# A fused two-layer matmul with scheduled fast products: nine sum slots in place of eight, 21 y slots in place of 23, new orders, and one block's x sums kept in DRAM for the second pass

## The chip, the cores and the metric

One core of one Trainium2 chip. The metric is the device time of one execution in microseconds (us), the median of the runs shown.

## The reference

```python
batch, m, k, h, n = 16, 512, 768, 3072, 768        # x, w1, b1, w2 in float32
y = np.maximum(np.matmul(x, w1) + b1, 0)
return np.matmul(y, w2).astype(np.float32)
```

With the batch flattened, x is 8192 x 768, w1 is 768 x 3072 and w2 is 3072 x 768.

## The kernel before

**Tiling.** The hidden dimension 3072 is cut into two *chunks* of 1536. Rows of x are cut into eight *blocks* of 1024. One *iteration* handles one block with one chunk: iterations 0 to 7 run chunk one over blocks 0 to 7, iterations 8 to 15 chunk two over blocks 7, 0, 1, ... 6 (`block`). Chunk one writes its part of the output to DRAM; chunk two adds its part there, with stores that accumulate, and only POOL's queue can issue those.

**Fast products.** Both layers use a bilinear scheme with fewer products than a plain split. Each operand is cut into pieces, sums and differences of pieces are formed first, products of these are taken, and the products are combined into the outputs. Stage one (`add_first`, matmuls at L980) multiplies sums of x by sums of w1: 40 products of six matmuls an iteration. The first block alone is done plainly (L890). Stage two (`add_second`, matmuls at L1109) multiplies sums of y by sums of w2: 26 products of six matmuls. The tables `X_SUMS`, `Y_SUMS`, `W1_SUMS` and `W2_SUMS` name each sum (result, two sources, sign), and `X_FUSE` and `Y_FUSE` say which two consecutive sums go as one DVE instruction of double width. `FIRST_ORDER` and `SECOND_ORDER` give the order of the products (`SWITCH_ORDER` for iterations 7 and 8, `LAST_ORDER` for the last one).

**After a product.** A chain of products ends in PSUM. It becomes an output ("out"), a *kept sum* in SBUF ("sum"), or the start of another chain in PSUM ("seed"). Where a chain stands alone, ACT copies it (L1016, L1020, L1120); where a kept sum is added, DVE does it (L1023, L1026, L1031, L1126). Kept sums of both stages, and outputs of stage two on their way to DRAM, share the slots of the tile `s`, `S_SLOTS` = 8 of 3 KB a partition. A slot is free again when the last reader is through, and for an output that is the landing of its store. The tile `y` has `Y_SLOTS` = 23 slots of 1.5 KB: 16 for the pieces of y and seven for sums; a further sum takes the slot of a sum or a piece whose last product is done (`place_between`).

**Split outputs.** An output that is a chain plus a kept sum can be made in two ways. Usually DVE adds the two (L1126) and one store is issued. Where it is *split* (`SPLIT` names output 6 always; `APART` names iterations, here 7 and 8, in which all such outputs are split), the kept sum is stored by itself (L1161), ACT copies the chain, and a second, accumulating store adds it (L1158).

**x.** POOL loads half a block of x with a cast to fp16 (L634, 768 KB), SP transposes it into x slots by DMA (`add_turns`, 8 a block), and DVE forms the x sums (L735). In the iteration in which a block's x is transposed, ACT squares its rows once for a range check (`add_square_x`, L694); similar squares check w1 and w2 (`add_stats`). At the end of the check one matmul counts the values in range (`add_check`), DVE makes a flag (L1281), and all engines read it for a branch behind the fast path.

**Order of the work.** `plan` adds every operation to a `Graph` with its engine, an assumed duration and what it reads and writes. `Graph.run` plays that through with these assumed durations and fixes for each engine the order in which its instructions are emitted; on the chip only data dependences remain. A task marked `idle` (squares) is put where the engine has room before its next urgent task. A store's `lat` is the time that the planner assumes until its slot is free. On each engine, POOL's and SP's DMA queues among them, instructions go strictly in the emitted order.

Of the kernel before, what the change touches and what calls it, by code (L numbers as in the profile page):

```python
# [10 lines left out]
FP16 = mybir.dt.float16  # L11
# [7 lines left out]
P = 128  # L19
# [11 lines left out]

X_SUMS = ((17, 6, 1, -1), (20, 7, 5, -1), (12, 2, 0, -1), (23, 4, 6, -1), (10, 3, 1, -1), (16, 1,
    0, -1), (21, 7, 1, -1), (8, 4, 5, -1), (15, 2, 1, -1), (14, 3, 5, -1), (11, 2, 5, -1), (22, 6,
    7, -1), (19, 4, 2, -1), (9, 6, 5, -1), (13, 0, 6, -1), (18, 3, 2, -1))
FIRST_U = (8, 9, 21, 18, 2, 13, 20, 19, 1, 14, 10, 17, 11, 22, 6, 12, 5, 23, 15, 16)
W1_SUMS = ((6, 2, 5, 1), (15, 3, 5, -1), (7, 0, 1, 1), (13, 7, 2, -1), (8, 6, 4, -1), (9, 6, 3,
    -1), (12, 9, 0, -1), (14, 7, 9, -1), (10, 8, 7, -1), (16, 3, 10, -1), (17, 1, 8, -1), (11, 5,
    4, -1))
FIRST_V = (2, 9, 4, 11, 17, 1, 3, 1, 16, 4, 3, 14, 8, 15, 12, 0, 6, 0, 10, 13)
# [28 lines left out]
FIRST_SEEDS = (16, None, None, 13, 12, 14, None, None, None)  # L68
FIRST_ORDER = (16, 20, 36, 0, 12, 4, 1, 24, 8, 7, 18, 28, 9, 15, 10, 21, 38, 3, 32, 35, 30, 27,
    14, 29, 34, 17, 37, 31, 23, 6, 11, 25, 26, 2, 5, 39, 13, 22, 19, 33)  # L70
SWITCH_ORDER = (36, 16, 20, 12, 4, 8, 9, 0, 7, 18, 28, 24, 15, 10, 21, 38, 3, 32, 35, 30, 27, 1,
    29, 14, 34, 37, 11, 31, 6, 17, 22, 25, 26, 23, 2, 5, 39, 13, 33, 19)

Y_SUMS = ((35, 6, 7, 1), (21, 1, 3, 1), (19, 10, 11, 1), (16, 0, 12, 1), (20, 8, 9, 1), (28, 2,
# [4 lines left out]
SECOND_U = (36, 38, 25, 27, 28, 3, 16, 23, 13, 11, 14, 39, 20, 35, 34, 17, 42, 41, 29, 33, 43, 40,  # L79
    18, 22, 32, 31)  # L80
W2_SUMS = ((18, 5, 1, -1), (9, 5, 7, -1), (10, 4, 5, -1), (12, 2, 0, -1), (23, 12, 9, -1), (11, 3,
    2, -1), (8, 2, 6, -1), (20, 9, 6, -1), (13, 1, 10, 1), (17, 1, 11, 1), (24, 11, 10, -1), (15,
    8, 3, -1), (14, 9, 1, -1), (16, 8, 0, -1), (22, 16, 4, -1), (25, 0, 13, 1), (19, 7, 15, -1),
    (21, 3, 14, -1))
SECOND_V = (8, 10, 13, 14, 16, 21, 22, 23, 1, 19, 6, 25, 4, 12, 3, 20, 11, 0, 15, 9, 4, 18, 17,
    24, 0, 7)
W2_NEG = (1, 6)
SECOND_OPS = {
    0: (1, 1, 9, 1, 'out', 2, None),
    1: (4, 1, 14, 1, 'out', 3, None),  # L90
    2: (0, 1, None, None, 'out', 0, None),
    3: (4, -1, 12, 1, 'out', 1, None),
    4: (2, -1, 11, 1, 'out', 4, None),
    5: (2, 1, 20, 1, 'out', 5, None),
    6: (3, 1, 19, 1, 'out', 6, None),
# [30 lines left out]
LAST_ORDER = (13, 15, 4, 17, 10, 12, 18, 8, 2, 0, 3, 14, 1, 19, 21, 23, 25, 11, 16, 7, 22, 9, 5,  # L126
    6, 24, 20)
# [3 lines left out]

X_FUSE = (0, 2)
Y_FUSE = (7, 9, 13, 18, 26)

S_SLOTS, Y_SLOTS = 8, 23

# [145 lines left out]
class Graph:  # L282
# [5 lines left out]
    ENGINES = ("PE", "DVE", "ACT", "POOL", "SP")  # L288
    HOLD = 2.0
    CROSS = {"PE": 0.15, "DVE": 0.08, "ACT": 0.08, "POOL": 0.1, "SP": 0.1}  # L290

# [87 lines left out]
    def run(self, begin=0.0, lookahead=0.2, ahead=5):  # L379
# [37 lines left out]
        while left:  # L417
            best = None
            for e in self.ENGINES:
                cands = []  # L420
                low = 1e9
                for t in avail[e]:
# [25 lines left out]
                    if t.idle and start < t.due + drift:  # L448
                        d = demand[e]
                        while first[e] < len(d) and d[first[e]].end is not None:  # L450
                            first[e] += 1
                        if first[e] < len(d) and start + t.ns > d[first[e]].late + drift + 0.3:
                            continue
# [60 lines left out]
SPLIT = (6,)  # L514
APART = (7, 8)

STATS = ((1, 2, 3, 4, 5, 6, 7), (2, 3, 4))


class Fast:  # L520
# [43 lines left out]
    def open(self, ctx, tc):  # L564
# [15 lines left out]
        self.w1dram = dram.tile([P, self.NG, 6, 3, 2 * P], FP16, name="w1d")  # L580
        self.w2dram = dram.tile([P, 8, 3, self.NH], FP16, name="w2d")


# [41 lines left out]
    def block(self, it):  # L625

        return it if it < self.NSB else (it - 1) % self.NSB

# [61 lines left out]
    def add_square_x(self, it, s, due=None):  # L690
        i = self.block(it) * 8 + s

        def square():
            self.nc.scalar.activation(out=self.xn[:, s, :], in_=self.xn[:, s, :],  # L694
                                      func=ACTF.Square,
                                      accum_out=self.stat[:, self.stat_at["x"] + i:][:, 0:1])
        self.g.add("ACT", 850, square, writes=[("xn", s), ("stat", "x", i)], due=due, idle=True)

# [76 lines left out]
    def add_stat_w1(self, c, g, i, after=()):  # L775
# [9 lines left out]
        for n in range(2):  # L785
            self.g.add("ACT", 935, lambda n=n: square(n), reads=[] if n else [("w1", g, slot)],
                       writes=["junk"] + ([("stat", "w1", at)] if n else []), idle=True,
                       after=after)

    def add_stat_w2(self, c, i, after=()):  # L790
        slot = self.w2s[c][i]
        for n, (h0, h1) in enumerate(((0, 2), (2, 3))):
            at = self.stat_at["w2"] + c * 16 + 2 * i + n

            def square(h0=h0, h1=h1, at=at):
# [3 lines left out]
                    accum_out=self.stat[:, at:at + 1])  # L799
            self.g.add("ACT", 520 if n else 935, square,  # L800
                       reads=[("w2", slot, h) for h in range(h0, h1)],
# [283 lines left out]
    def add_second(self, it):  # L1085
# [104 lines left out]
        for kind, n in steps:  # L1190
# [21 lines left out]
            if what == "out":  # L1212
# [9 lines left out]
                elif n in apart:  # L1222
                    assert b == 1
                    self.g.add("POOL" if c else "SP", 1375 if c else 100,
                               lambda to=to, u=u: store_sum(to, u), reads=[kept[u]],
                               writes=[("out", self.block(it), to)], lat=9.0 if it == 0 else 6.5)
                    engine = "ACT"
# [68 lines left out]
    def plan(self):  # L1296
# [51 lines left out]
    def iteration_end(self, it):  # L1348
# [4 lines left out]
        self.add_second(it)  # L1353
        if it + 1 < NIT and it + 1 != NSB:
            self.add_turns(it + 1)
            if (it + 1 < NSB) == (self.block(it + 1) > 1):
                for s in range(8):
                    self.add_square_x(it + 1, s)
            to = it + 2 + (it + 2 == NSB)
            if to < NIT:  # L1360
                for half in range(2):
                    self.add_load_x(to, half)
            self.add_x_sums()
        if it == NSB - 1:
            slot = self.w2s[1]
# [74 lines left out]
```

## Time and profile before

| | us |
|---|---|
| Median of 3 runs (lowest, highest) | 875.22 (874.09, 876.23) |
| The profiled execution's own time | 878.86 |
| Its span | 877.3 |
| TensorE (PE) busy | 852.7 |
| VectorE (DVE) busy | 755.1 |
| ScalarE (ACT) busy | 556.5 |
| GpSimd (POOL) busy | 154.5 |
| Stage one's matmuls (L980) busy | 399.7 |
| Stage two's matmuls (L1109) busy | 417.5 |
| DMA moved | 124.99 MB, mean 142 GB/s |

Busy times are unions of instruction times on one engine, in one profiled execution. Matmuls are pipelined, so a busy TensorE need not be at its peak. "Idle before" is an engine's idle time just before an instruction, and the name behind it is what ended it. A DMA's landing is counted from its issue.

### The profile page before, as it was taken

To read this page: it belongs to the slowest core of one execution; us is meant where nothing else is said; L and a number is where in the kernel's file an instruction comes from. 1 tells how busy PE (TensorE), PEld (TensorE's weight loads), DVE (VectorE), ACT (ScalarE), POOL (GpSimd) and SP (SyncE) were. 2 spreads that over 40 slices of the span, in tenths; PEclk is the share of its full clock that TensorE was granted. 3 is DMA by queue.
4 is the path that set the end of the run, shared out by engine and by line. 5 is a ranking of instruction groups with operands and counts; after the bars stand their busy time and mean duration, and the time that the engine had idled before them with its cause. 6 is when DMAs were issued, how large, how long until landed. Compare 5 with 4: busy or idle time off the path is not lost. (4 is left out here: it accounts for less than half of the span.)

```text
span 877.3 us, 16551 instructions
## 1 busy us (share of the span) xinstructions
PE 852.7 (97%) x6381; PEld 624.9 (71%) x6381; DVE 755.1 (86%) x1207; ACT 556.5 (63%) x1066; POOL 154.5 (18%) x168
## 2 busy tenths in 40 slices
PE   8999999999999999999999799999999999999996
PEld 7558778586776868778586575776858677586873
DVE  4899988979889898998989589799798988889896
ACT  5757857678576775847858467675856636355452
POOL 5210020201002010000113502314022140401301
PEclk9999999999999999999999999999999999999998
DMA  9994596875849576592976996989778896873827
GB/s 211 198 187 125 98 228 108 150 180 96 206 74 202 131 107 174 91 268 66 253 135 99 201 142 105 158 119 140 116 117 143 126 145 111 127 124 55 145 74 163
DMA packets 168247, 124.99 MB, mean 142 GB/s; under 512 B 93645, under 2 KB 166629, under 8 KB 168165
## 3 DMA queue, kind: packets, MB, share of 16 engines
q0 software_dynamic: 54928, 66.46, 49.1%
q1 hardware_dynamic: 112768, 56.45, 26.8%
q8 instruction: 50, 0.82, 0.4%
q10 hardware_dynamic: 468, 1.00, 0.3%
q14 instruction: 33, 0.26, 0.1%
HBM read 72.76 MB, written 66.06 MB: 158 GB/s over the span
## 5 line engine op out<-in xcount | busy, mean ns | idle before, releaser
L1109 PE MATMUL ps<-v,y 128*128 128x384 f16 x2496 | 417.5, 326 | 4.8 <-ACT s L1120 4.0
L980 PE MATMUL ps<-x,v 128*128 128x256 f16 x3600 | 399.7, 273 | 9.7 <-DVE ps L1031 5.8
L980 PEld LDWEIGHTS <-v 128*128 128x128 f16 x3600 | 352.3, 98 | 56.3 <-issue 14.1
L1109 PEld LDWEIGHTS <-y 128*128 128x128 f16 x2496 | 243.5, 98 | 174.3 <-issue 16.1
L953 DVE TENSOR_TENSOR y<-y 128x768 f16<-128x768 f16 (+1 forms) x368 | 225.4, 641 | 10.4 <-ACT y L899 0.2
L1023 DVE CUSTOM_DVE_ANT_0 y<-ps,s 128x512 f16<-128x512 f32 x240 | 159.2, 687 | 60.4 <-ACT s L1020 36.2
L1120 ACT ACTIVATE s<-ps 128x768 f32<-128x768 f32 x171 | 138.4, 810 | 93.4 <-PE ps L1109 80.4
L1020 ACT ACTIVATE s<-ps,bt 128x256 f32<-128x256 f32 x180 | 75.3, 472 | 80.7 <-PE ps L980 55.8
L735 DVE TENSOR_TENSOR x<-x 128x768 f16<-128x768 f16 (+1 forms) x196 | 113.4, 607 | 1.3 <-DVE x L735 1.0
L1158 POOL DMA_DIRECT2D out_dram<-s x73 | 88.0, 1412 | 145.8 <-ACT s L1120 90.6
L634 POOL DMA_DIRECT2D xn<-in_x_dram x30 | 23.6, 789 | 426.9 <-ACT xn L694 289.7
L1120 ACT ACTIVATE ps<-ps 128x768 f32<-128x768 f32 x80 | 63.6, 795 | 47.2 <-DVE s L1126 32.7
L1126 DVE TENSOR_TENSOR s<-ps,s 128x768 f32<-128x768 f32 x85 | 80.6, 957 | 5.9 <-PE ps L1109 3.2
L1020 ACT ACTIVATE y<-ps,bt 128x256 f16<-128x256 f32 x180 | 72.0, 474 | 16.3 <-PE ps L980 16.3
L1126 DVE TENSOR_TENSOR s<-s,ps 128x768 f32<-128x768 f32 x59 | 56.2, 952 | 8.5 <-PE ps L1109 8.0
L694 ACT ACTIVATE xn<-xn 128x768 f16<-128x768 f16 x64 | 53.5, 843 | 2.4 <-DMA x<-xn 2.4
L1016 ACT ACTIVATE ps<-ps 128x512 f32<-128x512 f32 x60 | 34.2, 591 | 27.1 <-DVE y L1023 26.9
L1020 ACT ACTIVATE ps<-ps,bt 128x256 f32<-128x256 f32 x60 | 26.7, 448 | 28.1 <-PE ps L980 26.9
L1161 POOL DMA_DIRECT2D out_dram<-s x14 | 17.1, 1300 | 126.4 <-ACT s L1120 126.4
L890 PE MATMUL ps<-x,v 128*128 128x256 f16 (+1 forms) x216 | 32.1, 308 | 1.0 <-DMA v<-in_w_dram 0.6
L1026 DVE SCALAR_TENSOR_TENSOR s<-ps,bt,s 128x256 f32<-128x256 f32 x60 | 26.2, 478 | 5.1 <-PE ps L980 3.0
L890 PEld LDWEIGHTS <-v 128*128 128x128 f16 x216 | 20.9, 98 | 11.4 <-DMA v<-in_w_dram 0.9
(58 smaller groups left out, 300.2 us busy)
## 6 DMA issues: line engine op xcount, KB each, us to landing
out_dram<-s POOLq DMA_DIRECT2D x87, 384.0 KB, 8.4
out_dram<-s SPq DMA_DIRECT2D x68, 384.0 KB, 6.6
xn<-in_x_dram POOLq DMA_DIRECT2D x28, 768.0 KB, 8.0
v<-in_w_dram POOLq DMA_DIRECT2D x6, 384.0 KB, 10.7
v<-in_w_dram POOLq DMA_DIRECT2D x12, 192.0 KB, 9.1
w1d<-in_w_dram POOLq DMA_DIRECT2D x6, 384.0 KB, 18.6
w2d<-in_w_dram POOLq DMA_DIRECT2D x12, 192.0 KB, 14.3
v<-w1d SPq DMA_DIRECT2D x12, 192.0 KB, 4.3
```

The costliest lines, as they stand in the source:

```text
L694: self.nc.scalar.activation(out=self.xn[:, s, :], in_=self.xn[:, s, :], func=ACTF.Square, accum_out=self.stat[:, self.stat_at["x"] + i:][: ...
L735: self.nc.vector.tensor_tensor(out=self.two(x, out), in0=self.two(x, in0), in1=self.two(x, in1), op=ALU.add if sign > 0 else ALU.subtract)
L890: nc.tensor.matmul(self.ps[:, ps.at[0], cols], lhsT=self.v1[:, gi, 2 * h + k2, k, j * P:(j + 1) * P], rhs=rhs, start=(k2 == 0 and k == 0), ...
L953: self.nc.vector.tensor_tensor(out=self.two(self.y, out), in0=self.two(self.y, in0), in1=self.two(self.y, in1), op=ALU.add if sign > 0 els ...
L980: nc.tensor.matmul(self.ps[:, at, j * self.QM:(j + 1) * self.QM], lhsT=self.v1[:, gi, self.w1s[c][gi][FIRST_V[p]], k, j * P:(j + 1) * P], ...
L1016: nc.scalar.activation(out=out, in_=ps, scale=float(a), func=func if kind == "out" else ACTF.Copy)
L1020: nc.scalar.activation(out=out[:, j], in_=ps[:, j], func=func, scale=float(a), bias=beta(j))
L1023: nc.vector._custom_dve(TENSOR_ADD_SAT, out=out, in0=ps, in1=s, s0=F_MAX, s1=0.0)
L1109: nc.tensor.matmul(self.ps[:, bank[ch].at[j], 0:NH], lhsT=self.y[:, ys[SECOND_U[p]], m0:m0 + P], rhs=self.v2[:, slot[SECOND_V[p]], h, :], ...
L1120: nc.scalar.activation(out=out, in_=ps, func=ACTF.Copy, scale=float(a))
L1126: engine.tensor_tensor(out=out, in0=in0, in1=in1, op=ALU.add if a == b else ALU.subtract)
L1158: nc.gpsimd.dma_start(out=rows, in_=out, accum_op=ALU.add)
```

## The change

- `S_SLOTS` 8 becomes 9, `Y_SLOTS` 23 becomes 21; the SBUF space is the same.
- New orders of the products, and of the sums of x, y, w1 and w2; the products and the operations stay the same but for names. `X_FUSE` loses one pair, so that a block's x sums are 15 instructions in place of 14; `Y_FUSE` has five pairs as before.
- `APART` becomes iterations 0 and 7.
- Chunk two runs over the blocks 7, 2, 0, 1, 3, 4, 5, 6. Block 2's x slots, pieces and sums, are stored to DRAM in iteration 1 (`add_keep_x`, 20 DMAs on SP) and loaded in iteration 8 (`add_kept_x`, 20 DMAs on SP), in place of its second load, transposes and sums. The x of iteration 10 is loaded at the end of iteration 6.
- The squares of blocks 0 and 1 fall into iterations 9 and 10 instead of 8 and 9. The checks of the weights in chunk two spread over four iterations instead of three, and the final count and the flag come one iteration later.
- The planner's assumed durations for squares and its assumed `lat` of stores are larger. `NEXT` = 1 looks at one urgent task, as before.

```diff
-X_SUMS = ((17, 6, 1, -1), (20, 7, 5, -1), (12, 2, 0, -1), ...
+X_SUMS = ((15, 2, 1, -1), (21, 7, 1, -1), (16, 1, 0, -1), ...
...
-FIRST_ORDER = (16, 20, 36, 0, 12, 4, 1, 24, 8, 7, 18, 28, ...
+FIRST_ORDER = (16, 0, 12, 36, 20, 8, 4, 7, 9, 1, 18, 24, ...
...
-SECOND_ORDER = (13, 15, 4, 17, 10, 8, 18, 12, 3, 0, 1, 2, 14, 23, 19, 21, 11, 25, 7, 16, 22, 5, 6,
-    9, 24, 20)
+SECOND_ORDER = (13, 15, 4, 17, 10, 8, 18, 12, 3, 0, 1, 14, 2, 19, 23, 21, 11, 16, 25, 7, 9, 22, 6,
+    5, 24, 20)
...
-X_FUSE = (0, 2)
-Y_FUSE = (7, 9, 13, 18, 26)
-S_SLOTS, Y_SLOTS = 8, 23
+X_FUSE = (0,)
+Y_FUSE = (7, 10, 12, 19, 25)
+S_SLOTS, Y_SLOTS = 9, 21
...
-APART = (7, 8)
-STATS = ((1, 2, 3, 4, 5, 6, 7), (2, 3, 4))
+APART = (0, 7)
+KEPT = (2,)
+SECOND_CHUNK = (7, 2, 0, 1, 3, 4, 5, 6)
+STATS = ((1, 2, 3, 4, 5, 6, 7), (2, 3, 4, 5))
...
-        return it if it < self.NSB else (it - 1) % self.NSB
+        return it if it < self.NSB else SECOND_CHUNK[it - self.NSB]
+    def kept(self, it):
+        return self.NSB < it < self.NIT and self.block(it) in KEPT
...
-        self.g.add("ACT", 850, square, ...
+        self.g.add("ACT", 1035, square, ...
+    def add_keep_x(self, it):
+        n = KEPT.index(self.block(it))
+        for a in self.x_slots():
+            self.g.add("SP", 100, lambda a=a: self.nc.sync.dma_start(
+                out=self.xdram[:, n, a], in_=self.x[:, a]), lat=4.0, ...
+    def add_kept_x(self, it):
+        n = KEPT.index(self.block(it))
+        for a in self.x_slots():
+            self.g.add("SP", 600, lambda a=a: self.nc.sync.dma_start(
+                out=self.x[:, a], in_=self.xdram[:, n, a]), lat=4.0, ...
...
-                           lat=9.0 if it == 0 else 3.5 if direct else 6.5)
+                           lat=3.5 if direct else 9.0)
...
-            if it == NSB + 5:
+            if it == NSB + 6:
                 later = self.add_check()
-            elif it == NSB + 6:
+            elif it == NSB + 7:
                 later()
-            elif it == NSB + 7:
                 g.add("SP", 10, self.load_flag, reads=["flag"])
...
-        if it + 1 < NIT and it + 1 != NSB:
+        if self.kept(it + 1):
+            self.add_kept_x(it + 1)
+        elif it + 1 < NIT and it + 1 != NSB:
             self.add_turns(it + 1)
...
-            to = it + 2 + (it + 2 == NSB)
+            to = [n for n in range(it + 2, NIT) if n != NSB and not self.kept(n)]
...
             self.add_x_sums()
+            if it + 1 < NSB and self.block(it + 1) in KEPT:
+                self.add_keep_x(it + 1)
```

More of the change, by code (lines that the diff above doesn't have):

```diff
@@ L451, in run @@
                             first[e] += 1
-                        if first[e] < len(d) and start + t.ns > d[first[e]].late + drift + 0.3:
+                        end, fits = start + t.ns, True
+                        for n in range(first[e], min(first[e] + self.NEXT, len(d))):
+                            if d[n].end is None:
+                                fits &= end <= d[n].late + drift + 0.3
+                                end += d[n].ns
+                        if not fits:
                             continue
@@ L696, in square, with x_slots @@
                                       accum_out=self.stat[:, self.stat_at["x"] + i:][:, 0:1])
-        self.g.add("ACT", 850, square, writes=[("xn", s), ("stat", "x", i)], due=due, idle=True)
+        self.g.add("ACT", 1035, square, writes=[("xn", s), ("stat", "x", i)], due=due, idle=True)
+    def x_slots(self):
+        last = {FIRST_U[p % len(FIRST_U)]: n for n, p in enumerate(FIRST_ORDER)}
+        return [self.xs[v] for v in sorted(last, key=lambda v: last[v])]
+    def add_keep_x(self, it):
+        n = KEPT.index(self.block(it))
+        for a in self.x_slots():
+            self.g.add("SP", 100, lambda a=a: self.nc.sync.dma_start(
+                out=self.xdram[:, n, a], in_=self.x[:, a]), lat=4.0,
+                reads=[("x", a, h) for h in range(2)], writes=[("xd", n, a)])
+    def add_kept_x(self, it):
+        n = KEPT.index(self.block(it))
+        for a in self.x_slots():
+            self.g.add("SP", 600, lambda a=a: self.nc.sync.dma_start(
+                out=self.x[:, a], in_=self.xdram[:, n, a]), lat=4.0, reads=[("xd", n, a)],
+                writes=[("x", a, h) for h in range(2)])
     def sums_of(self, table, slots, fused):
@@ L785, in add_stat_w1 @@
         for n in range(2):
-            self.g.add("ACT", 935, lambda n=n: square(n), reads=[] if n else [("w1", g, slot)],
+            self.g.add("ACT", 1040 if n else 845, lambda n=n: square(n), reads=[] if n else [("w1", g, slot)],
                        writes=["junk"] + ([("stat", "w1", at)] if n else []), idle=True,
@@ L1225, in add_second @@
                                lambda to=to, u=u: store_sum(to, u), reads=[kept[u]],
-                               writes=[("out", self.block(it), to)], lat=9.0 if it == 0 else 6.5)
+                               writes=[("out", self.block(it), to)], lat=9.0)
                     engine = "ACT"
```

58 lines of the change are left out of this document (30 added, 28 removed), and 8 rows, old and new, of the table Y_SUMS.

## The prediction

> **What bounds the kernel now.** I read the page, then TensorE's timeline over the span, the waits, ACT's and POOL's timelines where TensorE stops, busy time by stage, and the groups. In TensorE's rows the first number is the start, the bracket the idle time before and what ended it.
>
> ```profile
> span 877.3 us, 16551 instructions
> PE 852.7 (97%) x6381; PEld 624.9 (71%) x6381; DVE 755.1 (86%) x1207; ACT 556.5 (63%) x1066; POOL 154.5 (18%) x168
> 43.18 25.94 PE L1109 MATMUL ps<-v,y 128*128 128x384 f16 x156
> 68.95 8.90 PE L980 MATMUL ps<-x,v 128*128 128x256 f16 x78
> ...
> 135.83 13.91 PE L980 MATMUL ps<-x,v 128*128 128x256 f16 x126 [0.69 <-DVE ps L1031]
> ...
> 333.85 26.36 PE L980 MATMUL ps<-x,v 128*128 128x256 f16 x240
> 360.05 25.98 PE L1109 MATMUL ps<-v,y 128*128 128x384 f16 x156
> 385.88 26.36 PE L980 MATMUL ps<-x,v 128*128 128x256 f16 x240
> ...
> 464.96 14.40 PE L1109 MATMUL ps<-v,y 128*128 128x384 f16 x84
> 479.88 10.98 PE L1109 MATMUL ps<-v,y 128*128 128x384 f16 x66 [0.52 <-DVE y L953]
> 494.52 2.08 PE L1109 MATMUL ps<-v,y 128*128 128x384 f16 x6 [3.66 <-ACT s L1120]
> ...
> 527.10 25.94 PE L1109 MATMUL ps<-v,y 128*128 128x384 f16 x156
> 552.88 8.68 PE L980 MATMUL ps<-x,v 128*128 128x256 f16 x78
> ...
> 843.94 26.30 PE L1109 MATMUL ps<-v,y 128*128 128x384 f16 x156
> ```
>
> TensorE is the path, so what counts is by how much its stages exceed their undisturbed length. I write f6 for stage one (L980) of iteration 6, s6 for its stage two (L1109). The undisturbed f6 takes 360.05 - 333.85 = 26.20 us (40 products of 0.655), the undisturbed s6 25.83 (26 products of 0.993). From 43.18 to the last product's end, 843.94 + 26.30 = 870.24, lie 15 stages one and 16 stages two: 806.3 us undisturbed, 827.1 as measured. The 20.8 us between are gaps, and no new order can win more. By stretch: f1 to s5 (from 68.95) 264.90 - 5 x 52.03 = 4.75; f7 to f8 (from 385.88) 79.08 - 78.23 = 0.85; s8 and f9 (from 464.96) 62.14 - 52.03 = 10.11; f10 to f15 (from 552.88) 291.06 - 286.35 = 4.71; s15 0.47.
>
> ```profile
> ACT s L1020 <- DMA out_dram<-s: 23.9, 23, 2.6
> ACT s L1120 <- DMA out_dram<-s: 7.4, 4, 4.0
> 129.44 0.84 ACT L1020 ACTIVATE s<-ps,bt 128x256 f32<-128x256 f32 x2 [1.35 <-PE ps L980]
> 133.15 0.84 ACT L1020 ACTIVATE s<-ps,bt 128x256 f32<-128x256 f32 x2 [1.01 <-DMA out_dram<-s]
> 493.66 0.81 ACT L1120 ACTIVATE s<-ps 128x768 f32<-128x768 f32 x1 [4.00 <-DMA out_dram<-s]
> 495.58 0.81 ACT L1120 ACTIVATE s<-ps 128x768 f32<-128x768 f32 x1 [1.11 <-DMA out_dram<-s]
> ```
>
> Most gaps have one cause: ACT wants to write a sum into a slot of s whose store has not landed (the first two rows, from the waits: 31.3 us of ACT). The wait of 1.01 before 133.15 passes through DVE, which adds that sum, and becomes TensorE's 0.69 at 135.83. In s8, which splits its outputs, 15 accumulating stores and two x loads stand in POOL's queue; slots come free only 495.58 - 493.66 = 1.92 us apart, ACT stands for 4.00 and TensorE for 3.66. DVE is the next engine, at 86%.
>
> **The change, part by part.**
>
> ```profile
> 412.08:438.51 26.43, 25.95 (x158) 15.07 (x156) 24.83 (x43) 20.92 (x32) 4.09 (x4) 1.00 0.85 230
> 438.51:464.96 26.45, 26.36 (x243) 23.49 (x240) 24.09 (x39) 16.66 (x40) 4.38 (x4) 1.00 0.74 129
> 464.96:496.40 31.44, 27.17 (x159) 15.24 (x157) 27.16 (x42) 20.41 (x33) 13.61 (x12) 0.96 0.87 144
> ...
> L1126 DVE TENSOR_TENSOR s<-ps,s 128x768 f32<-128x768 f32 x85 | 80.6, 957 | 5.9 <-PE ps L1109 3.2
> L1120 ACT ACTIVATE s<-ps 128x768 f32<-128x768 f32 x171 | 138.4, 810 | 93.4 <-PE ps L1109 80.4 <-DMA out_dram<-s 7.4
> L1023 DVE CUSTOM_DVE_ANT_0 y<-ps,s 128x512 f16<-128x512 f32 x240 | 159.2, 687 | 60.4 <-ACT s L1020 36.2 <-PE ps L980 19.5 <-DVE s L1031 2.5
> L769 DVE TENSOR_TENSOR v<-v 128x1152 f16<-128x1152 f16 x36 | 25.7, 751 | 1.1 <-ACT v L759 0.6 <-DMA v<-in_w_dram 0.5
> L735 DVE TENSOR_TENSOR x<-x 128x768 f16<-128x768 f16 x168 | 89.2, 550 | 1.3 <-DVE x L735 1.0
> L735 DVE TENSOR_TENSOR x<-x 128x1536 f16<-128x1536 f16 x28 | 26.6, 950 | 0.0
> ...
> L1156 SPq DMA_DIRECT2D out_dram<-s x7: 372/372/373, 115.5 to 123.2; - x7
> DMA to landing us min/median/max: 6.9/8.0/10.7
> ```
>
> (The windows are s7, f8 and s8: length, then busy PE, PEld, DVE, ACT, POOL. The last two rows are the plain stores of s1.)
>
> *Ninth slot, new orders.* In the emitted order a slot's distance is the TensorE work between its store and its next user. Before, six slots of an ordinary stage one have 7.9 to 9.2 us. For the shortest, product 22 of stage two is followed by three more (2.98), its sum takes 0.957 to make, and the next user waits for nine products of the next stage one (5.90): 2.98 - 0.96 + 5.90 = 7.92. The stores need 6.9 to 10.7, so ACT waits. After, the four tightest have 10.6 to 12.5 (product 18 to the seventh: 6.95 - 0.96 + 4.59 = 10.58) and belong to the early stores of a burst, which land fastest; the late ones have over 13. Those waits go. What is late next is the chain without a slot, as at 129.44, where ACT waited for TensorE itself, for 0.2 to 0.3 a stage. I take 0.3 for f3, f4 and f5 together, and 0.9 for f10 to f14, where the x loads now stand among the stores of s9 and s10 in POOL's queue.
>
> *Outputs split in iteration 0, not 8.* A split output is copied by ACT (0.81) and its kept sum stored by itself, where DVE (0.957) added the two. In s8 six accumulating stores leave POOL (15 to 9; at 1.92 us 17.3 us of queue in a stage of 25.83), ACT loses 4.9 us, DVE gains 5.7; in s0 the reverse. Iteration 8's two x loads go as well.
>
> *Block 2's x kept.* Iteration 8 has no transposes and no x sums: DVE loses 12 x 0.55 + 2 x 0.95 = 8.5 us. Its 20 loads of 192 KB wait on SP for x slots that f8 frees, and nothing else is queued on SP behind them; all of s8 is their cover, and without it f9's first products would wait. By counts from the emitted order DVE's work in f8 becomes 24.09 + 1.0 = 25.1 of 26.20 (one 0.687, one 0.751 and two y sums come, two w1 sums of about 0.55 go). In s8 it stays 27.2, of 25.83: five sums of 0.957 come; four x sums, a 0.751, a 0.687 and two y sums go, while one y sum more is a double one. So 1.3 us of s8 may show. f9 is 4.9 lighter, and I leave it 0.7: s8 and f9 go from 10.11 to 2.0, f7 to f8 from 0.85 to 1.2. f1 is 5.7 lighter on DVE, but behind seven accumulating stores of s0; I take 0.6.
>
> *Keeping it.* In iteration 1 20 stores of 192 KB go onto SP, seven of them among the output stores of s1. Those output stores now land 1.9 us apart (seven issued over 7.7, the last landing 3.8 slower than the first: 11.5 over six steps), so half a store is 0.95. The store after product 22 gets six copies ahead of it: 8.0 + 6 x 0.95 = 13.7 against 12.5 of distance, late by 1.2. I take 1.1 for f2. Bounds: 0.2, where the copies cost nothing, and 8.0 + 6 x 1.9 - 12.5 = 6.9, where each takes as long as a whole store. The Trainium skill, DMA: Bandwidth & Descriptors, "Queues, rings and completion order", says that a DMA engine works through one ring in order and turns between rings packet by packet. By that rule all six stand ahead, and f2 loses the 1.2 and not the 0.2; the landings that slow from 6.9 to 10.7 within one burst agree with it.
>
> *21 y slots.* A y sum waits for the product that frees its slot. Behind such a wait at least four products now lie before its user (seven before): 4 x 0.993 covers a double sum, but not a DVE queue ahead of it. Bounds: nothing, or one late sum of 0.55 a stage. I take 0.8 over all ordinary stages two, since they show no gap now.
>
> *At nothing:* x sums unfused (15 instructions for 14, 0.15 us a block) under DVE's slack in stage one; the planner's costs, which only order; the squares of block 0 moved an iteration on, in ACT's idle time (63% busy). If that slack is gone, the 0.15 shows 13 times, 2 us. The check's flag halts TensorE once, for 0.90 between these rows of the chain of waits, in f14 now and in f15 after:
>
> ```profile
> 765.42 0.06 DVE flag L1281
> 765.49 0.48 DVE x L735
> 765.96 0.90 issue
> 766.87 25.05 PE ps L980 x228
> ```
>
> **Sum.** f1 0.6, f2 1.1, f3 to f5 0.3, f7 to f8 1.2, s8 and f9 2.0, f10 to f14 0.9, flag 0.9, stages two 0.8, s15 0.5: 8.3 us of gaps in place of 20.8, so 12.5 less in the profiled execution, 878.86 - 12.5 = 866.4. (Of its 878.86, 877.3 are span.) The median of the runs, 875.22, lies 3.64 lower; whether those 3.64 are gaps isn't shown. If they are, 17.2 of 20.8 remain to win from and the gain is 12.5 x 0.83 = 10.3; that is the value I take: 865.0, with 861 to 869 as its own range.
>
> **Rivals.** (1) All slot gaps go and nothing comes in their place; left are the flag's 0.9, f7 to f8's 0.85, s15's 0.47 and 1.0 of chains: 3.2. Gain 17.6 x 0.83 = 14.6, 860.6. For it: the 31.3 us of ACT's waits. Against: 129.44, and the kept copies. The Trainium skill, Perfetto Trace Analysis, "Optimization Strategy", reads a gap that repeats on the engine that should be saturated as a sign of too few buffers; by it this would be the case, and the trace agrees but for that row. Chance 0.13. (2) In s8 DVE takes POOL's place: the six sums that return (5.7) stand on the path, gain (12.5 - 5.7) x 0.83 = 5.6, 869.6. For it: 27.2 of work in 25.83. Against: the x sums that could be late after them are gone. f2 at its upper bound gives nearly the same. Chance 0.17. (3) Slower: with two y slots fewer TensorE waits for y sums in every stage two, as for the 0.52 at 479.88. With two late sums of 0.55 a stage that is 16 x 1.1 = 17.6 above the forecast, 882.6; from 10.3 / 16 = 0.64 a stage it is slower than before. For it: DVE is busy 24.83 of 26.43 in s7. Against: ordinary stages two have no gap, though the trace doesn't size their slack. Chance 0.12. (4) The change does not act: the queues, not the slots, set the pace, stores land later by as much as the distances grow, and the 10 us of s8 come back in f1 and f2: 875. Chance 0.06.
>
> **How the numbers follow.** Forecast 0.52; faster 0.52 + 0.13 + 0.17 = 0.82, same 0.06, slower 0.12, with the bound at 0.2% (1.75 us, about what a measurement of this kernel tells from no change). The range, 859.5 to 874, takes in the first three cases and leaves out the slower one and the last.
>
> **What would show it.** Right: s8 under 27.5 and f9 under 27.0 long, ACT's waits for stores under 10 us in place of 31.3, f3 and f10 at 26.2 to 26.6. Wrong: gaps ended by y sums (DVE y L953) in many stages two, f2 over 30, or f9's first products waiting for kept x.

## The result, and the profile after

The changed kernel takes 878.84 us (median of 20 runs, 875.72 to 884.3), the kernel before, on the same chip, 875.88 (20 runs, 873.42 to 878.3): a ratio of 1.0038, 95% interval 1.0026 to 1.005. It is slower by 0.4%, a small difference but clear of the noise, where 865.0 was forecast. The profiled execution took 878.07. From its page the span and the busy times, from TensorE's timeline the stages with gaps (L1013 is stage one now, L1142 stage two), and from the waits the four that matter:

```profile
span 876.5 us, 16636 instructions
PE 850.6 (97%) x6381; PEld 625.0 (71%) x6381; DVE 744.5 (85%) x1206; ACT 557.8 (64%) x1066; POOL 154.7 (18%) x166
```
```profile
70.89 1.47 PE L1013 MATMUL ps<-x,v 128*128 128x256 f16 x12 [0.72 <-ACT s L1153]
73.83 2.12 PE L1013 MATMUL ps<-x,v 128*128 128x256 f16 x18 [1.47 <-ACT s L1153]
78.31 21.77 PE L1013 MATMUL ps<-x,v 128*128 128x256 f16 x198 [2.35 <-ACT ps L1049]
...
137.59 3.43 PE L1013 MATMUL ps<-x,v 128*128 128x256 f16 x30 [1.07 <-DVE y L1056]
141.43 2.78 PE L1013 MATMUL ps<-x,v 128*128 128x256 f16 x24 [0.40 <-DVE ps L1064]
145.99 8.68 PE L1013 MATMUL ps<-x,v 128*128 128x256 f16 x78 [1.78 <-ACT ps L1049]
157.16 1.47 PE L1013 MATMUL ps<-x,v 128*128 128x256 f16 x12 [2.49 <-DVE y L1056]
...
409.98 10.64 PE L1013 MATMUL ps<-x,v 128*128 128x256 f16 x96 [2.63 <-DVE ps L1064]
...
475.75 20.13 PE L1142 MATMUL ps<-v,y 128*128 128x384 f16 x120
496.26 2.11 PE L1142 MATMUL ps<-v,y 128*128 128x384 f16 x12 [0.39 <-DVE v L802]
498.69 4.31 PE L1142 MATMUL ps<-v,y 128*128 128x384 f16 x24 [0.31 <-ACT ps L1153]
502.83 26.36 PE L1013 MATMUL ps<-x,v 128*128 128x256 f16 x240
529.03 21.14 PE L1142 MATMUL ps<-v,y 128*128 128x384 f16 x125
```
```profile
ACT s L1053 <- DMA out_dram<-s: 8.9, 3, 3.8
DVE x L768 <- DMA x<-xn: 8.0, 6, 4.5
ACT s L1153 <- DMA out_dram<-s: 4.6, 3, 2.1
DVE v L784 <- DMA v<-w1d: 3.7, 1, 3.7
```

The place that the prediction aimed at is nearly clean: s8 is 27.08 long (502.83 - 475.75) in place of 31.44, f9 26.20 without a gap, ACT's waits for stores fall from 31.3 us to 13.5 (DVE's rise from 1.8 to 5.2). What came in their place stands in three stages: f1 (4.54 in the three gaps shown), f2 (5.74 in the four) and f7 (2.63). The table adds up, for each stage, its length from TensorE's rows less the undisturbed 26.20 or 25.83; "other" is the rest of the stages two without s2, s7 and s8.

| us | f1 | f2, s2 | f3-f5 | f6 | f7-f8 | s8, f9 | f10-f14 | f15 | other | sum |
|---|---|---|---|---|---|---|---|---|---|---|
| before | 1.08 | 1.32 | 2.39 | 0.00 | 0.85 | 10.12 | 4.30 | 0.15 | 0.57 | 20.78 |
| forecast | 0.6 | 1.1 | 0.3 | | 1.2 | 2.0 | 0.9 | 0.9 | 1.3 | 8.3 |
| changed | 5.02 | 6.99 | 0.21 | 0.00 | 4.31 | 1.26 | 0.65 | 0.33 | 1.72 | 20.48 |

So 14.7 us of gaps went (f3 to f5, s8 and f9, f10 to f14) and 13.1 came in f1, f2, s2, f7 and f8 (s7 is counted with these two); the rest is in the small columns. The prediction had read every wait from the side of the engine that stands. Of the DMA engines it showed only the mean share of a stage (0.74 to 0.87 in s7, f8 and s8). Here they are for the 36 us around f2 of the changed kernel: busy share (a 9 is 90% or more) and GB/s in 40 slices, then the two kinds of queue (software: POOL's; hardware: SP's) with packets, MB and share of the 16 engines, then the issues with KB each and median landing:

```profile
DMA  9999999999999999999999999999999999999999
GB/s 155 152 169 251 249 260 350 382 271 254 253 261 256 259 266 279 286 283 283 287 289 282 288 287 282 284 293 279 286 279 291 273 285 279 236 191 139 96 193 266
q1 hardware_dynamic: 6475, 6.14, 62.6%
q0 software_dynamic: 4171, 3.09, 57.2%
...
out_dram<-s SPq DMA_DIRECT2D x6, 384.0 KB, 12.7
xd<-x SPq DMA_DIRECT2D x12, 192.0 KB, 10.9
w1d<-in_w_dram POOLq DMA_DIRECT2D x4, 384.0 KB, 23.3
```

Every slice is full: packets are under way all the time, at anything from 96 to 382 GB/s. Before the change the engines were full in this place too, but only until 135 us (115 to 150 us):

```profile
DMA  9999999999999999999999974930009569670669
```

f2 began at 122.05 there and begins at 125.88 here, so the engines stayed full for 13 us of it and now do for 30. The copies of block 2's x sums stand in the same stretch as the output stores of s1, an x load, and four staging loads of the second chunk's w1 (L627, float32 to fp16, DRAM to DRAM). POOL issued these before the change too, there from 111.3 to 113.8, ahead of the plain stores of s1, and here from 123.5 to 125.9, among them. The stores of s1, which landed after 8.0 us (median), take 12.7. The transposes for iteration 3 come last of all: the first goes out at 146.8 and lands at 155.0, DVE's x sums wait up to 4.5 for them, and TensorE 2.49 at 157.16. The first experiments set the order in the queues (theory Q) against DVE's work (theory D); the later ones test **the rate** against the order in SP's queue. The rate says that at each of the three places the change puts so many bytes into one stretch that all 16 DMA engines stay full, and whatever is last there is late. Another rival, which the result suggested, is that the slots were never the limit.

### The profile page after: what moved, and what is told of

It reads as the page before. It is cut to its first block, busy times and chain, and to the rows that moved or that the text cites. A ratio compares the mean times of both kernels' runs of the same rounds, so it can differ in the third digit from the quotient of the medians.

```text
span 876.5 us, 16636 instructions
## 1 busy us (share of the span) xinstructions
PE 850.6 (97%) x6381; PEld 625.0 (71%) x6381; DVE 744.5 (85%) x1206; ACT 557.8 (64%) x1066; POOL 154.7 (18%) x166
## 3 DMA queue, kind: packets, MB, share of 16 engines
q0 software_dynamic: 53872, 64.89, 46.8%
q1 hardware_dynamic: 112128, 62.74, 28.4%
## 5 line engine op out<-in xcount | busy, mean ns | idle before, releaser
L1142 PE MATMUL ps<-v,y 128*128 128x384 f16 x2496 | 416.8, 326 | 2.3 <-ACT ps L1153 0.7
L1013 PE MATMUL ps<-x,v 128*128 128x256 f16 x3600 | 398.1, 273 | 14.0 <-ACT ps L1049 4.1
L1013 PEld LDWEIGHTS <-v 128*128 128x128 f16 x3600 | 352.1, 98 | 59.0 <-issue 16.7
L1142 PEld LDWEIGHTS <-y 128*128 128x128 f16 x2496 | 243.7, 98 | 171.4 <-issue 15.0
L986 DVE TENSOR_TENSOR y<-y 128x768 f16<-128x768 f16 (+1 forms) x368 | 222.4, 639 | 6.6 <-DVE y L1056 0.5
L1191 POOL DMA_DIRECT2D out_dram<-s x79 | 95.5, 1419 | 141.6 <-ACT s L1153 62.7
L768 DVE TENSOR_TENSOR x<-x 128x768 f16<-128x768 f16 (+1 forms) x195 | 108.1, 577 | 9.2 <-DMA x<-xn 8.0
L1053 ACT ACTIVATE y<-ps,bt 128x256 f16<-128x256 f32 x180 | 72.1, 475 | 46.8 <-PE ps L1013 46.7
L648 POOL DMA_DIRECT2D xn<-in_x_dram x28 | 21.6, 775 | 395.5 <-ACT xn L708 294.5
L1064 DVE TENSOR_TENSOR s<-s,ps 128x512 f32<-128x512 f32 x30 | 20.5, 682 | 14.7 <-PE ps L1013 13.4
L1064 DVE TENSOR_TENSOR ps<-s,ps 128x512 f32<-128x512 f32 x30 | 20.8, 695 | 12.3 <-PE ps L1013 9.1
L784 DVE TENSOR_TENSOR v<-v 128x768 f16<-128x768 f16 x48 | 24.7, 552 | 6.9 <-DMA v<-w1d 3.7
```

Source lines behind the costliest of these rows:

```text
L768: self.nc.vector.tensor_tensor(out=self.two(x, out), in0=self.two(x, in0), in1=self.two(x, in1), op=ALU.add if sign > 0 else ALU.subtract)
L986: self.nc.vector.tensor_tensor(out=self.two(self.y, out), in0=self.two(self.y, in0), in1=self.two(self.y, in1), op=ALU.add if sign > 0 els ...
L1013: nc.tensor.matmul(self.ps[:, at, j * self.QM:(j + 1) * self.QM], lhsT=self.v1[:, gi, self.w1s[c][gi][FIRST_V[p]], k, j * P:(j + 1) * P], ...
L1053: nc.scalar.activation(out=out[:, j], in_=ps[:, j], func=func, scale=float(a), bias=beta(j))
L1064: nc.vector.tensor_tensor(out=out, in0=in0, in1=in1, op=ALU.add if a == b else ALU.subtract)
L1142: nc.tensor.matmul(self.ps[:, bank[ch].at[j], 0:NH], lhsT=self.y[:, ys[SECOND_U[p]], m0:m0 + P], rhs=self.v2[:, slot[SECOND_V[p]], h, :], ...
```

## The experiments

Gaps by stage as in the table above, from one profiled execution each; "start" is when s0 begins. The ratio is that of the medians of all runs, to runs of the kernel before on the same chip.

| us | start | f1 | f2, s2 | f6 | f7-f8 | s8, f9 | all gaps | time, ratio to before [95%] |
|---|---|---|---|---|---|---|---|---|
| changed | 42.9 | 5.02 | 6.99 | 0.00 | 4.31 | 1.26 | 20.48 | 1.0038 [1.0026, 1.005] |
| before again | 43.0 | 1.08 | 1.11 | 0.00 | 0.85 | 10.24 | 19.58 | one run |
| nothing kept | 43.0 | 6.55 | -0.01 | 0.00 | 4.24 | 5.27 | 19.28 | 0.9995 [0.9983, 1.0007] |
| no split in 0 | 44.3 | 2.29 | 7.70 | 0.00 | 7.32 | 1.28 | 21.84 | 1.0002 [0.9988, 1.0016] |
| w1 loads by ACT | 42.9 | 5.10 | 8.81 | 0.00 | 5.35 | 1.25 | 25.58 | 1.0047 [1.003, 1.0064] |
| x load in 8 | 43.1 | 6.35 | 7.58 | 0.00 | 1.34 | 1.26 | 19.92 | 0.9995 [0.9983, 1.0007] |
| copies after stores | 43.0 | 4.81 | 9.39 | 0.00 | 5.56 | 1.26 | 24.35 | 1.0059 [1.0041, 1.0077] |
| three at once | 44.7 | 2.29 | 8.88 | 0.00 | 1.34 | 1.28 | 17.19 | 0.9973 [0.9961, 0.9986] |
| copies by POOL | 43.2 | 6.72 | 6.25 | 0.00 | 3.95 | 1.57 | 23.70 | 1.0038 [1.0022, 1.0055] |
| block 6 kept | 44.7 | 4.75 | -0.01 | 1.99 | 5.57 | 1.26 | 17.39 | 0.998 [0.9968, 0.9992] |
| staging later | 43.3 | 6.38 | 0.45 | 0.00 | 4.02 | 1.26 | 16.80 | 0.9952 [0.9933, 0.9971] |
| eight slots | 43.0 | 6.40 | 6.63 | 0.46 | 9.72 | -0.01 | 41.03 | 1.0273 [1.0254, 1.0293] |
| three repairs | 43.4 | 2.29 | -0.01 | 1.13 | 1.34 | 1.28 | 9.58 | 0.9886 [0.9867, 0.9905] |

Where f1's code is the changed kernel's, f1 measured 4.75 to 6.72: a difference of 2 us there between two of these kernels means nothing. The same holds for f2 with s2 (6.99 to 8.81 where nothing there was edited) and for differences of 3 us in f7 to f8 (3.95 to 7.32 likewise). Nor does "start" in these runs: it is 1.4 to 1.8 longer in three kernels, and why stays open.

**Before again.** The kernel before, unchanged.

> The kernel before, unchanged, for a second profile. The profiled execution of before took 878.86 us where the median of 20 runs is 875.88, so about 3 us of its gaps may not be typical. If the waits for slots in s8 and f9 vary from execution to execution, s8 plus f9 (10.11 us over their undisturbed 52.03) should come out 2 to 4 us smaller here, and f1 to s5 and f10 to f15 within 1 us of 4.75 and 4.71. If the 3 us lie elsewhere (the start, the end, every stage a little), s8 plus f9 stays at 10 and the undisturbed stages or the first 43 us are shorter.

877.51 us, in a span of 875.9, beside a median of 877.47 on that chip. Its gaps are 19.58 us, in the same places as in the first profile (s8 and f9 10.24 of them). So the 20 us are the kernel's own.

**Nothing kept.**

```diff
-KEPT = (2,)
+KEPT = ()
```

> The changed kernel, but block 2's x is loaded, transposed and summed again in iteration 9, nothing is kept. Theory Q (queues): the 20 stores of 192 KB stand on SP's queue among and ahead of iteration 1's output stores, and SP has eight DMAs under way at most, so they make f2 (32.58 us in the changed kernel) and s2 (26.44) long; f2 falls to 26.2 to 26.8, s2 to 25.9. Nothing is gained back in iteration 8 but 0 to 2 us in f9, which gets its x sums again. Time 5 to 7 us under the changed kernel's 878.84, 872 to 874. Theory D (DVE): the new orders themselves overload DVE in f1, f2 and f7; then f2 stays over 30 and the time does not fall, or rises with the 8.5 us of x sums in iteration 8.

f2 has no gap left, and f9 gets 4.01, its first products waiting for x sums in DVE (1.52 of them below). The ratio falls from 1.0038 to 0.9995, which is 3.8 us, where 5 to 7 were expected.

```profile
503.66 3.45 PE L1013 MATMUL ps<-x,v 128*128 128x256 f16 x30 [1.52 <-DVE x L768]
```

Keeping block 2 therefore wins 4.0 us, all of them in f9 (s8 keeps 1.26 with it and without), and costs 7.0 in f2 and s2.

**No split outputs in iteration 0.**

```diff
-APART = (0, 7)
+APART = (7,)
```

> The changed kernel with outputs split in iteration 7 alone: in iteration 0 DVE adds six kept sums again (5.7 us more DVE work in s0 and f1) and the seven accumulating stores are gone. Theory Q: f1 is 31.22 us long because the stores of kept sums share the DMA engines with two x loads and land after 11 to 15 us, against distances of 8.1 to 10.7; without the split they are issued late in s0 behind the x loads as before, and f1 falls to 26.5 to 27.5; time 3.5 to 5 us less, 874 to 875. Theory D: f1 becomes longer by up to 5 us, since DVE has more to do there; time 879 to 884.

f1 falls to 2.29 (28.49 long, where 26.5 to 27.5 were expected). The queues over 23 us at the end of s0 and the start of f1, first of the changed kernel (57 to 80 us), then without the split (58 to 81):

```profile
q0 software_dynamic: 2022, 2.96, 74.2%
q1 hardware_dynamic: 1963, 2.82, 38.3%
...
out_dram<-s SPq DMA_DIRECT2D x5, 384.0 KB, 11.9
```
```profile
q0 software_dynamic: 1094, 1.61, 39.1%
q1 hardware_dynamic: 2012, 2.89, 35.2%
...
out_dram<-s SPq DMA_DIRECT2D x7, 384.0 KB, 3.2
```

With the accumulating stores of the split outputs POOL's queue holds the engines for 74.2% of this stretch in place of 39.1%, and SP's stores, which free the slots, land in 11.9 in place of 3.2. Part of that is when they go out: the kept sums of split outputs are stored from 51.3 us on, beside two x loads of which the last lands at 66.5, and the whole outputs of this run from 63.7 on. The run takes both away at once and doesn't tell them apart. The time follows: the ratio falls from 1.0038 to 1.0002, about 3 us. The profiled execution, 3.1 us above the median of this kernel, hides it by a longer f7 (f7 to f8 7.32) and start (44.3).

**The w1 loads by ACT.** The 12 loads of the second chunk's w1 for f7, from ACT's queue in place of SP's.

```diff
-                    g.add("SP", 100, lambda gi=gi, ...: self.nc.sync.dma_start(
+                    g.add("ACT", 400, lambda gi=gi, ...: self.nc.scalar.dma_start(
```

> The changed kernel, but chunk two's twelve loads of w1 in iteration 7 are issued by ACT (about 0.4 us of ACT each, 5 us in f7, where ACT has 9 us free) instead of SP. Theory Q: f7 is 29.65 us long because these loads stand on SP behind output stores that land after 9 us, each waiting until the DMA eight places earlier has landed, and DVE's queue holds a w1 sum that waits 3.67 us for one of them; on ACT's own queue they go earlier, and f7 falls to 26.3 to 27.2; time 2.5 to 3.3 us less, 875.5 to 876.5. Theory D, or one by which all DMAs share the same rate whatever queue issues them: the loads land as late as before and f7 stays at 29 to 30.

```profile
405.80 3.44 PE L1013 MATMUL ps<-x,v 128*128 128x256 f16 x30 [1.91 <-DVE ps L1064]
411.05 12.61 PE L1013 MATMUL ps<-x,v 128*128 128x256 f16 x114 [1.81 <-ACT ps L1049]
```

f7 keeps 4.70, in two larger gaps in place of one. ACT stood for 5.3 us, because the third load of this row could not be issued until a store that SP had issued at 393.50, eight DMAs before, had landed at 403.73; the copies of finished chains stood behind it:

```profile
399.12 5.01 ACTq L1363 DMA_DIRECT2D v<-w1d  x3
```

So the loads wait for SP's stores on ACT's queue too, and now ACT waits with them. The stores between 388 and 412 us land no sooner than before this edit:

```profile
out_dram<-s SPq DMA_DIRECT2D x7, 384.0 KB, 10.9
```

Another queue is no remedy here. Whether the loads would have come in time without that wait, this run can't say, since it did not free them from it.

**The x load for iteration 10, two iterations later.** In the changed kernel it is issued at the end of iteration 6, among the stores of s6, and the w1 loads follow.

```diff
-            to = [n for n in range(it + 2, NIT) if n != NSB and not self.kept(n)]
+            to = [] if it == NSB - 2 else [n for n in range(it + 2, NIT) if ...]
...
+        if it == NSB:
+            for half in range(2):
+                self.add_load_x(it + 2, half, [g.last_pe])
```

> The changed kernel with one transfer moved: the x of iteration 10 is loaded in iteration 8 (behind stage one on POOL's queue) and not at the end of iteration 6. Putting the w1 loads on ACT's queue had left f7 at 30.9 us, so it is not SP's queue alone. Theory R (rate): two x loads, seven output stores and twelve w1 loads share the DMA engines around the end of s6; without the two x loads the stores land in 4 to 7 us instead of 9 to 12, the w1 loads follow at once, and f7 falls from 29.65 to 26.2 to 27.2; iteration 8 has room on POOL's queue, f9 loses 0 to 1; time 2 to 3.5 us below the changed kernel (1.0038 of before becomes 0.9998 to 1.0015). Rival (order): DVE's queue holds a w1 sum too early, whatever the DMA does; f7 stays over 29.

f7 falls from 3.45 to 0.66, to a length of 26.86, inside the 26.2 to 27.2 of the rate. The output stores between 388 and 412 us, first in the changed kernel, then with the load moved:

```profile
out_dram<-s SPq DMA_DIRECT2D x6, 384.0 KB, 9.2
v<-w1d SPq DMA_DIRECT2D x12, 192.0 KB, 5.7
xn<-in_x_dram POOLq DMA_DIRECT2D x1, 768.0 KB, 10.8
```
```profile
out_dram<-s SPq DMA_DIRECT2D x7, 384.0 KB, 2.8
v<-w1d SPq DMA_DIRECT2D x12, 192.0 KB, 4.1
```

**The copies behind the stores.** From the ninth on, the copies of the x sums go onto SP only after the output stores of s1.

```diff
-                out=self.xdram[:, n, a], in_=self.x[:, a]), lat=4.0,
+                out=self.xdram[:, n, a], in_=self.x[:, a]), lat=4.0, after=[] if a < 8 else [
+                    self.g.writer[("out", self.block(it - 1), to)] for to in range(8)],
```

> The changed kernel with one order changed: of the 20 stores that keep x, those of the twelve x sums stand on SP behind iteration 1's output stores (all but a few piece copies), not among them. Theory W (window): a DMA of SP is issued only when the one eight places earlier has landed, so the copies hold the output stores back at the issue as well as in the ring; behind them they hold nobody but the transposes for iteration 3. f2 falls from 32.58 to 26.2 to 27.5, s2 stays at 25.9 to 27 with late transposes; time 4 to 7 us below the changed kernel (0.996 to 0.999 of before). Theory R (rate alone): the bytes are the same, so f2 stays over 30.

A plain miss for theory W: f2 is 34.26 long, as the rate expected (over 30), and f2 and s2 lose 9.39, no less than without the edit. No sum waits for a store in f2 any more. Its four gaps become one, of y pieces that stand in DVE behind an x sum, which waits 8.7 us for its transpose behind the copies:

```profile
157.46 2.72 PE L1014 MATMUL ps<-x,v 128*128 128x256 f16 x12 [6.70 <-DVE y L1057]
```

The order in the queue chooses who is late; it doesn't take the lateness away.

**Those three at once** (no split in 0, copies behind the stores, x load in 8).

> The changed kernel with three repairs together: outputs split in iteration 7 alone, copies of x sums behind the output stores, the x of iteration 10 loaded in iteration 8. If the three places add up: f1 5.0 to 2.3, f2 and s2 7.0 to 1.0, f7 3.4 to 0.6, so 11.5 us of the 20.5 us of gaps go and the kernel takes 0.989 to 0.992 of before. If they trade with one another (what one frees another takes), 0.995 to 1.0.

f1 and f7 to f8 repeat what the single edits gave (2.29 and 1.34), f2 and s2 stay at 8.88.

**The copies by POOL**, from its queue in place of SP's (`self.nc.gpsimd.dma_start`).

> The changed kernel with the 20 stores that keep x issued by POOL, at the same places in the order, instead of SP. The bytes and the time at which they are wanted are the same; only the queue differs. Theory W (SP's window and ring): f2 falls from 32.58 to under 28, since SP's stores no longer stand behind copies. Theory R (rate): stores and copies share the engines, f2 stays at 30 to 33. POOL's own queue carries two x loads and four w1 loads there, which land later; if that reaches the transposes of iteration 3, s2 or f3 grows by 1 to 3.

f2 and s2 keep 6.25, and s1 loses 1.27 besides. The loss keeps its size and changes its kind. Sums in f2 wait 1.5 us for stores, where the changed kernel has 9.9. But the copies now stand ahead of the four staging loads in POOL's queue and hold them back to 141.6 to 144.0 us. There they run beside the transposes, the first three of which land after 9.2, 7.7 and 6.3 us in place of the usual 2.8. So this edit moved two things, and the total stayed.

**Block 6 kept.** Iteration 6's staging has two loads of 192 KB in place of four of 384 KB.

```diff
-KEPT = (2,)
-SECOND_CHUNK = (7, 2, 0, 1, 3, 4, 5, 6)
+KEPT = (6,)
+SECOND_CHUNK = (7, 6, 0, 1, 2, 3, 4, 5)
```

> The changed kernel, but block 6 is kept in place of block 2, so that chunk two runs over 7, 6, 0, 1, 2, 3, 4, 5. The 20 copies then stand in s5 and f6, where the staging of the second chunk's weights has two loads of 192 KB, and not in s1 and f2, where it has four of 384 KB. Theory of the rate (the DMA engines are full, at 258 GB/s from 120 to 156 us, because copies, stores, x load and staging fall together): f2 has no gap (0 to 0.5), and f6 loses what is left over, 7.0 less 1.18 MB at 0.26 MB/us = 4.5, so 0 to 2.6 us; time 0.4 to 0.8% under the changed kernel. Rival (the copies' places in SP's order make the loss wherever they stand): f2 clean, f6 loses 6 to 8, no difference in time.

f2 is clean, and f6 loses 1.99, inside the 0 to 2.6 of the rate and far from the 6 to 8 of SP's order.

**The staging loads later.** Block 2 stays kept and SP's copies are untouched; only POOL's staging of the weights moves out of f2.

```diff
-        if 2 <= it <= 6:
-            for n in range((it - 2) * 4, min((it - 1) * 4, 18)):
+        if 3 <= it <= 6:
+            for n in range((it - 3) * 5, min((it - 2) * 5, 18)):
```

> The changed kernel, with block 2 kept, but the 18 staging loads of the second chunk's weights go five to an iteration into iterations 3 to 6 (before, four to an iteration from iteration 2). SP's queue and the copies are untouched. Theory of the rate: 1.57 MB less in f2, at 0.26 MB/us 6 us less of full DMA, so f2 and s2 lose 0 to 3 us in place of 7.0, and f3 to f6 stay under 0.5 each; time 0.4 to 0.8% under the changed kernel. Rival (SP's order): f2 and s2 lose 6 to 8 as now.

The same 36 us as above (120 to 156), without the four staging loads:

```profile
DMA  9999999999999999999999999981065976976986
GB/s 205 200 143 142 198 249 253 278 384 374 261 251 258 256 251 266 333 393 398 399 401 398 398 394 394 396 307 41 3 129 109 197 136 114 190 147 110 181 152 113
q1 hardware_dynamic: 9685, 6.93, 63.9%
q0 software_dynamic: 1250, 1.85, 30.2%
...
xd<-x SPq DMA_DIRECT2D x12, 192.0 KB, 5.9
```
```profile
138.47 15.88 PE L1013 MATMUL ps<-x,v 128*128 128x256 f16 x144 [0.30 <-DVE y L1056]
```

(The last row is TensorE's only gap in f2.) f2 and s2 fall from 6.99 to 0.45. The engines are full until 144 us only, the last copies land 0.5 us apart in place of 0.95, and the first transpose lands at 148.0 in place of 155.0, though all the copies are still there. This is the run that decides for f2: SP issues the same DMAs in the same order, and the loss went. Nor was it the order in POOL's queue: in the changed kernel the x load stands ahead of the four staging loads, and it lands after 12.1 us there and after 11.9 here.

**Eight slots.**

```diff
-S_SLOTS, Y_SLOTS = 9, 21
+S_SLOTS, Y_SLOTS = 8, 21
```

> The changed kernel with eight slots of s in place of nine; orders, 21 y slots and all else as changed. If the ninth slot is what took the waits for stores away: the shortest distance of an ordinary stage one is 8.6 us in place of 10.6, ACT's waits for stores come back to 25 to 35 us, f3 to f5 lose 0.4 to 1.0 each, f9 to f15 4 to 8 together, time 0.5 to 1.2% above the changed kernel. If the new orders alone did it: f3 to f5 under 0.3 each and no difference in time.

Both sides were wrong in part, and the ratio of 1.0273 is 2.3% above the changed kernel's, where 0.5 to 1.2% were expected. With the new orders f3 to f6 hardly need the ninth slot (0.46 together; before the change f3 to f5 lost 2.39). In f10 to f14 they need it badly: 11.51, and f15 4.05, more than the kernel before ever lost there. There the stores accumulate and land in POOL's queue one behind the other, and the longest waits for them are DVE's:

```profile
DVE s L1059 <- DMA out_dram<-s: 11.6, 4, 4.8
```
```profile
570.76 19.95 PE L1013 MATMUL ps<-x,v 128*128 128x256 f16 x180 [2.63 <-DVE s L1059]
```

The orders were made for nine slots, so this prices the slot within them, not the slot in the kernel before (whose orders need the 23 slots of y; that half of the change could not be tried alone).

**Three repairs**, one for each place: block 6 kept, no split in iteration 0, the x load for iteration 10 in iteration 8.

> The changed kernel with three edits at once, one for each place where the gain went: block 6 kept in place of block 2, no split outputs in iteration 0, and the x load for iteration 10 moved from the end of iteration 6 to iteration 8. Theory of the rate: f1 2.3, f2 0 to 0.5, f6 0 to 2.6, f7 0.7, f8 0.7, s8 1.3, f9 to s15 2.5 to 4: gaps of 8.5 to 11 us in place of 20.5, time 0.8 to 1.2% under the kernel before. Rival (SP's order): f6 loses 6 to 8, time 0.3 to 0.6% under the kernel before.

```profile
span 866.1 us, 16627 instructions
```
```profile
123.60 26.36 PE L1013 MATMUL ps<-x,v 128*128 128x256 f16 x240
149.80 25.99 PE L1142 MATMUL ps<-v,y 128*128 128x384 f16 x156
```

868.26 us beside 878.15, 0.9886 (0.9867 to 0.9905): faster than both kernels, and inside the 0.8 to 1.2% of the rate. The gaps are 9.58 in place of 20.48 (8.5 to 11 expected), f6 loses 1.13, and f2 is its undisturbed 26.20 (149.80 - 123.60).

## Why the prediction was wrong

**What held.** The slots: f3 to f5, s8 with f9, and f10 to f14 lost 2.12 together where 3.2 were forecast, and were 16.81 before. s8 kept 1.26 where 1.3 was worked out from DVE's work, but that is luck: DVE was busy for 24.65 us of s8 and not for 27.2, only one of the two gaps shown there is ended by DVE (v L802), and with the x sums back in iteration 8 (nothing kept) s8 keeps the same 1.26. The copies' benefit in f9 is real: without them it loses 4.01. The 21 y slots cost nothing that shows: the waits name one of 0.2 us for a y sum (DVE y L986) on TensorE's side in the whole run, so rival (3) had the sign and the wrong mechanism.

**The step that failed first: "Keeping it".** It followed one store with six copies ahead of it, at 0.95 us each, and came to 1.1 for f2. f2 and s2 lost 6.99. The price itself held: beside the staging loads the last copies land 0.95 apart, and s1's stores after 7.9 to 13.8, where 13.7 was worked out. (The 1.9 behind it counts seven landings, of which the trace has six, 2.1 apart; that is a small thing.) What it left out is all else that the copies put back while the staging and x loads fill the same engines. The later stores of s1 were issued late as well, some only when a copy eight places ahead had landed, and sums waited 9.9 us for them, to which the first three gaps of f2 lead back. The transposes come behind all 20 copies, not behind six: the first lands 29.2 us after f2 begins, where it was 16.0 before, and the fourth gap of f2 (2.49) is theirs; that of s2 (0.59) follows from it. The upper bound of 6.9 was right in size and only by accident, since it too followed one store. Moving the copies behind the stores did not help (9.39), giving them to another queue left the loss (6.25), and taking the staging loads away took it away (0.45). The rule that the prediction leaned on is about the order within a ring; the Trainium skill, DMA: Bandwidth & Descriptors, "Issuing engines are not separate DMA queues", is the one that bore on this case: whichever engine issues a DMA, it ends on the same 16 DMA engines. The run with the copies by POOL agrees (6.25 against 6.99). That with the w1 loads by ACT (4.70 in f7 against 3.45) is no test of it, since the loads kept waiting for SP's stores.

**The second: "f1 ... I take 0.6".** The seven accumulating stores of s0 were named and not priced, although s8 had the price beside it (slots 1.92 apart, a wait of 4.00). Splitting was counted as work taken from POOL in s8, not as the same work put into a stretch with two x loads. f1 lost 5.02; without the split 2.29. How much of that is the engines' time and how much the earlier stores, no run separated.

**The third: "f7 to f8 from 0.85 to 1.2".** Here only DVE's sums were counted. That the x load for iteration 10 moves to the end of iteration 6 stood in the list of changes, and its DMAs were not followed: they slowed the stores to 9.2 and the w1 loads behind them. f7 to f8 lost 4.31, with the load elsewhere 1.34.

Without these three terms the forecast has 5.4 us of gaps and the changed kernel 4.16. With the three places repaired the whole is 9.58 against 8.3. So the sum came out near where slots were the limit, and it left out the resource that became one. **Rival (4)** came nearest (875, with the 10 us of s8 back in f1 and f2), and got the place right, at a chance of 0.06; but the slots did set the pace where it said they did not.

**The scale.** The factor of 0.83 for the median, which lay 3.64 below the profiled execution, is not borne out: the second profile of before ran at its chip's median and still had 19.58 us of gaps.

## What to carry to other kernels

When a change moves or adds a transfer, read the DMA engines' own view for the stretch it goes to: if that keeps them full until something is needed, its bytes are paid by whatever lands last. Here neither another queue nor another order in the queue helped; moving bytes to another stretch did. A freed resource invites the next one: count each stage's transfers after the change, staging and background loads too, before a gap is booked as won. Where a gain vanishes, a table of gaps by stage finds where it went before any theory does.

## What the hardware showed

**POOL's transfers, most of them casting or accumulating, held the engines longer for their bytes.** Over the whole span of the changed kernel POOL's queue moved 64.89 MB in 46.8% of the engines' time, SP's 62.74 MB in 28.4%: 6.3 and 4.0 us of all 16 engines for a MB (0.468 x 876.5 / 64.89, and 0.284 x 876.5 / 62.74).

```profile
q0 software_dynamic: 53872, 64.89, 46.8%
q1 hardware_dynamic: 112128, 62.74, 28.4%
```

A casting load's bytes are counted as they are written: half a block of x is 512 x 768 values, 768 KB at two bytes. The shares count the time of packets, and packets of both queues are under way together (62.6% and 57.2% around f2), so these are not prices of a transfer by itself. Around f2 the engines move 273 to 293 GB/s in all while SP's stores and copies run beside the staging loads, and 393 to 401 while they run alone (the rows of both kernels are above).

**SP's DMAs hold each other up eight places apart.** In the changed kernel a store is issued at 126.21, and the copy issued eight places before it had landed at 126.13; the same at 131.54 and 131.48, at 134.00 and 133.94, and with a store eight places before at 129.99 and 129.89. So a slow landing also delays the issue eight DMAs on. With the w1 loads by ACT the places count over both queues: ACT issues loads at 403.81 and 405.71, and the stores that SP issued eight DMAs before them landed at 403.73 and 405.69. From the waits of SP's queue:

```profile
SPq L721 <- DMA out_dram<-s: 6.8, 5, 1.6
SPq L1189 <- DMA xd<-x: 4.0, 3, 2.0
```

With the copies on POOL, SP issues the last four stores of s1 between 1.7 us before and 1.2 us after f2 begins, in place of 0.3 to 8.1 after, and the waits for them in f2 fall from 9.9 to 1.5. f2 and s2 kept 6.25 all the same, because the transposes then paid. So the delay is part of what made the stores late, and no run shows what it costs by itself.
